# Four buffers instead of three for the split weights of a hybrid encoder layer, and half the transfer scratch

## The chip, the cores and the metric

The kernel runs on one core of a Trainium2 chip. The metric is the device time of one execution in microseconds (us). Beside it there is one profiled execution, whose trace is what the views below are taken from.

## What is computed

One layer of an encoder trunk, for 384 rows: 256 of a new stream and 8 × 16 of running streams. The model width is 2048.

```python
u = rmsnorm(x, g_mix_pre)
proj = u @ w_in                     # columns: pool | z | xBC | dt | gates
a_pool = pool_mixer(pool_in, ...)   # windows 2, 4, 8, 16, then pool_w
a_ssd = gated_rmsnorm(ssd_scan(causal_conv(xbc), ...), z, ssd_norm)
merged = gate_A * (a_pool @ w_pool_proj) + gate_B * (a_ssd @ w_ssd_proj)
x = x + rmsnorm(merged @ w_out, g_mix_post)
hdn = square(relu(rmsnorm(x, g_mlp_pre) @ w_up)) @ w_down
x = x + rmsnorm(hdn, g_mlp_post)
```

The new pool, convolution and scan states are outputs too.

## The kernel before

**Split products.** Every weight and every activation is float32 and is multiplied as a sum of a high part and a low part, both in the type float32r. `mm3` (L101 to L104) makes three matmuls of each product: high weight by high activation, high by low, low by high. So each weight unit of 128 × 1024 numbers goes through three steps. SyncE (SP) loads it into a raw tile `w` (`wfetch`, L64). ScalarE (ACT) writes the rounded copy `wh` (L71 in `wsplit`). VectorE (DVE) writes the rest, `wl` = `w` − `wh` (L72). `split` (L1206, L1207) does the same for the units of the two block products below, whose raw tiles come from another pool; `esplit` (L351, L353) does it for the first weights, and `chained` (L1753, L1754) for two units at the start of the last stage.

**Rings.** `wpool` holds three rings, `w`, `wh` and `wl`, each of three tiles of 4096 bytes in every partition. A tile can be written again only when its last reader is done. So `wh` and `wl` of unit n+3 wait for the last matmul of unit n, and `w` of unit n+3 waits for the DVE subtraction of unit n.

**Stages, in the order of time.** The projections of the pool part, the z part and the convolved x, B and C parts (`proj`, PSUM tiles `pj_p`, `pj_x`, `pj_z`), in eight rounds with the chunked scan between them. Their results go through two PSUM banks in turn (`mm` tiles), from which DVE reads them: `cbuf` (L436) for x, `zs` (L1099) for z. Then the two gates (`ga`, `gb`; `moving`, matmuls L155 to L157), with the block products `sq` of w_pool_proj and w_ssd_proj woven between their units. Then `wo` (w_out), then the MLP: `pj_up` (w_up) with the block products `wd` (w_down) woven in.

**Block products.** `quad` multiplies a 2 × 2 block of weight units with seven products instead of eight. Its seven forms are worked off in the order b11, b21, U, b22, W, V, X (L1259 to L1261 are the matmuls). U, W and X are sums of units. GpSimd (POOL) makes the first of these sums by a load that accumulates (L1219); DVE makes three more (L1246, `w_b` ← `w_b`, `w_b`). Partial sums are kept in `acc`: ACT copies them into a PSUM bank before the form that adds to it (L1231) and out again after it (L1236); DVE reads the others (L1238) and works off sums of finished blocks (L1286).

**Order.** The order of the instructions on each engine is fixed when the program is built. A scheduler places them by what they depend on, so that the number of tiles in a ring also moves instructions. `later` and `behind` keep some instructions behind the latest split.

Of the kernel before, what the change touches and what calls it, by code (L numbers as in the profile page):

```python
# [7 lines left out]
F32R = mybir.dt.float32r  # L8
# [6 lines left out]
P = 128  # L15
# [9 lines left out]
WINDOWS = (2, 4, 8, 16)  # L25
MAGIC = 1597463007.0
NWARM = 6

C_IDENT, C_ONES, C_MASK, C_CM, C_BM = 0, 128, 256, 768, 1024
C_RC, C_SCAN, C_END = 1032, 1096, 1504  # L30
# [3 lines left out]
def build(ctx, tc, io):  # L34
    nc = tc.nc
# [3 lines left out]
    wpool = ctx.enter_context(tc.tile_pool(name="wpool", bufs=3))  # L39
# [13 lines left out]
    def sstile(name):  # L53
        return pss.tile([P, 512], F32, tag="ss", name=name)

    def behind(ins):
        return nullcontext() if ins is None else tc.issue_after(ins.ins)
# [3 lines left out]
    def wfetch(src, name):  # L61
        w = wpool.tile([P, 1024], F32, tag="w", name=f"w_{name}")
        with behind(ahead[0]):
            fetched[0] = sy.dma_start(w, src)  # L64
        return w, name

    def wsplit(f):
        w, name = f
        h = wpool.tile([P, 1024], F32R, tag="wh", name=f"wh_{name}")
        l = wpool.tile([P, 1024], F32R, tag="wl", name=f"wl_{name}")  # L70
        cut[0] = s.activation(h, w, AF.Copy)  # L71
        cut[1] = v.tensor_tensor(l, w, h.bitcast(F32), ALU.subtract)  # L72
        return h, l
# [9 lines left out]
    def wload(src, name):  # L83
        return wsplit(wfetch(src, name))
# [204 lines left out]
    wt = sstile("warm_o")  # L289
    for _ in range(NWARM):  # L290
        te.matmul(wt, warm[:, :P], warm, start=True, stop=True)
# [30 lines left out]
    def xsplit(k):  # L322
        x = xr[k]
        h = xgp.tile([P, T], F32R, name=f"xgh{k}")
        l = xgp.tile([P, T], F32R, name=f"xgl{k}")
        g1 = x0[:, k : k + 1]
        s.activation(h, x, AF.Copy, scale=g1)
        xg.append((h, l))
        return v.scalar_tensor_tensor(
            out=l, in0=x, scalar=g1, in1=h.bitcast(F32), op0=ALU.mult, op1=ALU.subtract  # L330
        )
# [5 lines left out]
    def esplit(k):  # L337
        w = eu[k]
        n = 1 if k < 4 else 2
        h = wpool.tile([P, 1024], F32R, tag="wh", name=f"wh_e{k}")[:, : n * 512]  # L340
        l = wpool.tile([P, 1024], F32R, tag="wl", name=f"wl_e{k}")[:, : n * 512]
        hv, lv = (h, l) if n == 1 else (a.rearrange("p (k n) -> p k n", k=2) for a in (h, l))
        xl = None
        if k < 2:
            m = (P, 256)[k]
            with behind(low[0]):
                v.tensor_copy(hv[:, :m], w[:, :m])
            xl = xsplit(k)
            turn[0] = s.activation(hv[:, m:], w[:, m:], AF.Copy)
        else:  # L350
            turn[0] = s.activation(hv, w, AF.Copy)  # L351
        with behind(xl):
            low[0] = v.tensor_tensor(lv, w, hv.bitcast(F32), ALU.subtract)  # L353
        return h, l
# [25 lines left out]
    for k in range(4):  # L380
        if k > 1:
            xsplit(k)
        eprod(k, 0, esplit(k))
    for k in range(4, KD, 2):
        xsplit(k)
        xsplit(k + 1)
        hl = esplit(k)
        eprod(k, 0, hl)
        eprod(k + 1, 1, hl)
        if k in (10, 14):  # L390
            square((k - 10) // 4, turn[0])
    ps4 = sstile("pj_p4")[:, :T]
    early.append(ps4)
    half(ps4, 0, wsplit(f0), xg)
    square(2, None)
    half(ps4, 1, wsplit(f1), xg)
    dgh = pa.tile([P, 3, P], F32R, name="dgh", bufs=1)
    dgl = pa.tile([P, 3, P], F32R, name="dgl", bufs=1)
# [49 lines left out]
    with tc.tile_pool(name="phc", bufs=1, reuse_waits="tile") as pc, tc.tile_pool(name="phc2", bufs=2, reuse_waits="tile") as pc2:  # L448
# [5 lines left out]
        bufs = []  # L454
# [746 lines left out]
        return acc[:, nb // 2 * 9 + LEFT[b, nb % 2], :]  # L1201

    def split(w, name):
        h = wpool.tile([P, 1024], F32R, tag="wh", name=f"wh_{name}")
        l = wpool.tile([P, 1024], F32R, tag="wl", name=f"wl_{name}")
        cut[0] = s.activation(h, w, AF.Copy)  # L1206
        cut[1] = v.tensor_tensor(l, w, h.bitcast(F32), ALU.subtract)  # L1207
        return h, l

    def quad(nm, pool, acc, np_, fresh, unit, part, extra=lambda i: None, seeded=SEEDED):  # L1210
# [29 lines left out]
        def ready(f):  # L1240
            if f == ORDER[0] and not kept:
                load()
            wh, wl = split(kept[f], f"{f}_{nm}")
            if f in AHEAD:
                n, o, x, y, op = AHEAD[f]
                v.tensor_tensor(kept[o], kept[x], kept[y], op)  # L1246
                kept[n] = kept[o]
            return wh, wl
# [323 lines left out]
    with tc.tile_pool(name="phf", bufs=1, side="right", reuse_waits="tile") as pf, tc.tile_pool(  # L1572
        name="phf2", bufs=2, side="right", reuse_waits="tile"
# [9 lines left out]
        def act(fn):  # L1583
            with behind(ca[0]):
                ca[0] = fn()

        def dve(fn):
            with behind(cd[0]):
                cd[0] = fn()
# [158 lines left out]

        def chained(src, name):
            w, _ = wfetch(src, name)  # L1750
            h = wpool.tile([P, 1024], F32R, tag="wh", name=f"wh_{name}")
            l = wpool.tile([P, 1024], F32R, tag="wl", name=f"wl_{name}")
            act(lambda: s.activation(h, w, AF.Copy))  # L1753
            dve(lambda: v.tensor_tensor(l, w, h.bitcast(F32), ALU.subtract))  # L1754
            return h, l
# [37 lines left out]
        prod((0, 1), (6, 7))  # L1793
        prod((0,), range(8, 16))
        uw.append(chained(io["w_up"][1, 1], "up1_1"))
        prod((1,), range(8, KD))
        chain[0] = False
        for b, i in ((1, 2), (1, 3), (2, 0), (2, 1), (2, 2), (2, 3)):
            square(b, i)
        for b in range(3):  # L1800
            gp.dma_start(x1_scr[b], x1[:, b, :])
        u20 = chained(io["w_up"][2, 0], "up2_0")
        dgh = pf.tile([P, 3, P], F32R, name="dgh2")
        dgl = pf.tile([P, 3, P], F32R, name="dgl2")
# [21 lines left out]
    with tc.tile_pool(name="phg", bufs=1, side="right", reuse_waits="tile") as pg, tc.tile_pool(  # L1826
        name="phg2", bufs=2, side="right", reuse_waits="tile"
# [72 lines left out]
        for G4 in range(2 * NC):  # L1900
# [5 lines left out]
            for f4 in range(4):  # L1906
                f = G4 * 4 + f4
# [38 lines left out]
        for src, name in wd_units(3):  # L1946
            w, _ = wfetch(src, name)
            h = pg2.tile([P, 1024], F32R, tag="ff", name=f"eh_{name}", bufs=2)
            l = pz.tile([P, 1024], F32R, name=f"el_{name}")
# [3 lines left out]
        for b in range(3):  # L1953
            t = slice(b * P, b * P + P)
            for i in range(2):
                for k in range(4):
                    wh, wl = kept[i * 2 + k // 2]
# [141 lines left out]
```

## Time and profile before

| | us |
|---|---|
| median of three runs (lowest, highest) | 2579.84 (2579.22, 2581.45) |
| the profiled execution's own time | 2579.85 |
| its span, first to last instruction | 2578.1 |
| TensorE matmuls busy | 2562.9 |
| VectorE busy | 2031.0 |
| ScalarE busy | 1696.9 |
| GpSimd busy | 466.5 |

The span is 1.75 us shorter than the time of the same execution. PE is TensorE's matmuls and PEld its weight loads, DVE is VectorE, ACT ScalarE, POOL GpSimd, SP SyncE. In a timeline row stand the start in the span, the time taken, the engine, the line, what is written ← what is read and, in brackets, how long the engine had been idle and what ended that. A PE row's length is that of a pipelined matmul: the next one starts before it ends.

### The profile page before, as it was taken

The page shows a single profiled execution, that of the slowest core. Times are in us where ns is not written, and L with a number is a line of the kernel's source. Part 1 is how long each engine was busy: PE and PEld are TensorE (multiplying, and loading weights), DVE is VectorE, ACT ScalarE, POOL GpSimd, SP SyncE. Part 2 cuts the span into 40 slices and gives each one's busy share as a digit, 9 for nine tenths or more (in the row PEclk, how much of TensorE's full clock was granted, in tenths as well). Part 3 has the DMA queues.
Part 4 walks back from the last instruction along what each step waited for, and adds up shares of the span by engine and source line. Part 5 has one row for each costly group of instructions (what it writes and reads, how often), then busy time and mean ns, then how long its engine had stood idle before and what let it go on. Part 6 is the DMA issues. An engine that isn't in the chain of part 4 may idle for free.

```text
span 2578.1 us, 40110 instructions
## 1 busy us (share of the span) xinstructions
PE 2562.9 (99%) x14953; PEld 2387.1 (93%) x14953; DVE 2031.0 (79%) x2843; ACT 1696.9 (66%) x2683; POOL 466.5 (18%) x695
## 2 busy tenths in 40 slices
PE   9999999999999999999999999999999999999998
PEld 9999999999999988888888888999999999999997
DVE  6887889999999966898888855767777776777778
ACT  6545666666666546868888634666766666666665
POOL 0113445444544412211111100000000000000000
PEclk9999999999999999999999999999999999999999
DMA  7666767676767659977666545654555554555544
GB/s 286 207 220 224 238 218 231 216 242 224 232 216 244 225 181 313 290 233 218 199 189 200 189 168 191 211 157 147 156 160 167 166 161 148 155 157 166 159 156 155
DMA packets 150098, 516.57 MB, mean 200 GB/s; under 512 B 22432, under 2 KB 25312, under 8 KB 144656
## 3 DMA queue, kind: packets, MB, share of 16 engines
q1 hardware_dynamic: 98944, 355.14, 41.2%
q0 software_dynamic: 43904, 144.07, 19.3%
q10 hardware_dynamic: 7056, 14.81, 1.8%
q8 instruction: 117, 1.92, 0.3%
q14 instruction: 77, 0.63, 0.1%
HBM read 453.57 MB, written 60.36 MB: 199 GB/s over the span
## 4 chain that ended last, share of the span: by engine, by line
PE 91%; DVE 4%; issue 2%; ACT 1%; DMA 1%; POOL 0%; SPq 0%; DVEq 0%; ACTq 0%; POOLq 0%
PE pj_up L102 6%; PE pj_up L104 6%; PE pj_up L103 6%; PE wd L1260 6%; PE wd L1261 6%; PE wd L1259 6%; PE pj_x L102 5%; PE pj_x L103 5%; PE pj_x L104 5%; PE pj_z L104 3%; PE pj_z L103 3%; PE pj_z L102 3%; PE sq L1260 3%; PE sq L1261 3%; PE sq L1259 3%
## 5 line engine op out<-in xcount | busy, mean ns | idle before, releaser
L71 ACT ACTIVATE wh_up<-w_up 128x1024 fp32r<-128x1024 f32 x126 | 133.1, 1057 | 219.6 <-PE pj_up L103 202.5
L102 PE MATMUL pj_x<-xgh,wh_x 128*128 128x384 f32 x768 | 251.9, 328 | 0.9 <-DVE zs L1099 0.9
L102 PE MATMUL pj_up<-x1h,wh_up 128*128 128x384 f32 x768 | 250.5, 326 | 0.0
L103 PE MATMUL pj_x<-xgl,wh_x 128*128 128x384 f32 x768 | 250.4, 326 | 0.0
L104 PE MATMUL pj_x<-xgh,wl_x 128*128 128x384 f32 x768 | 250.4, 326 | 0.0
L103 PE MATMUL pj_up<-x1l,wh_up 128*128 128x384 f32 x768 | 250.4, 326 | 0.0
L104 PE MATMUL pj_up<-x1h,wl_up 128*128 128x384 f32 x768 | 250.4, 326 | 0.0
L72 DVE TENSOR_TENSOR wl_up<-w_up,wh_up 128x1024 fp32r<-128x1024 f32 x126 | 153.9, 1222 | 54.9 <-ACT wh_up L71 54.8
L1219 POOL DMA_DIRECT2D w_b_wd<-w_down x30 | 25.3, 843 | 832.9 <-DMA w_b_wd<-w_down 414.0
L102 PE MATMUL pj_z<-xgh,wh_z 128*128 128x384 f32 x512 | 166.9, 326 | 0.0
L103 PE MATMUL pj_z<-xgl,wh_z 128*128 128x384 f32 x512 | 166.9, 326 | 0.0
L104 PE MATMUL pj_z<-xgh,wl_z 128*128 128x384 f32 x512 | 166.9, 326 | 0.0
L102 PEld LDWEIGHTS pj_x<-xgh,wh_x 128*128 128x128 f32 x768 | 145.1, 189 | 3.1 <-DVE zs L1099 1.4
L103 PEld LDWEIGHTS pj_up<-x1l,wh_up 128*128 128x128 f32 x768 | 145.2, 189 | 1.2
L102 PEld LDWEIGHTS pj_up<-x1h,wh_up 128*128 128x128 f32 x768 | 145.2, 189 | 1.2
L103 PEld LDWEIGHTS pj_x<-xgl,wh_x 128*128 128x128 f32 x768 | 145.2, 189 | 0.0
L104 PEld LDWEIGHTS pj_x<-xgh,wl_x 128*128 128x128 f32 x768 | 145.2, 189 | 0.0
L104 PEld LDWEIGHTS pj_up<-x1h,wl_up 128*128 128x128 f32 x768 | 145.2, 189 | 0.0
L1236 ACT COPY acc<-wd 128x512 f32<-128x512 f32 x214 | 124.7, 583 | 23.8 <-PE wd L1261 23.8
L71 ACT ACTIVATE wh_x<-w_x 128x1024 fp32r<-128x1024 f32 x96 | 100.4, 1051 | 60.6 <-PE pj_z L103 30.1
L1259 PE MATMUL wd<-wh_b_wd,fh 128*128 128x512 f32 x360 | 136.4, 379 | 0.0
L1260 PE MATMUL wd<-wl_b_wd,fh 128*128 128x512 f32 x360 | 136.4, 379 | 0.0
(495 smaller groups left out, 8169.0 us busy)
## 6 DMA issues: line engine op xcount, KB each, us to landing
w_up<-w_up SPq DMA_DIRECT2D x128, 512.0 KB, 4.0
w_b_wd<-w_down SPq DMA_DIRECT2D x120, 512.0 KB, 4.2
w_x<-w_in SPq DMA_DIRECT2D x96, 512.0 KB, 4.0
w_z<-w_in SPq DMA_DIRECT2D x64, 512.0 KB, 4.2
w_b_sq<-w_ssd SPq DMA_DIRECT2D x64, 512.0 KB, 5.1
w_ga<-w_ga SPq DMA_DIRECT2D x32, 512.0 KB, 3.4
hs<-ssm POOLq DMA_DIRECT2D x16, 1024.0 KB, 6.2
new_ssm_s<-hs POOLq DMA_DIRECT2D x16, 1024.0 KB, 4.2
```

Source lines behind the costliest of these rows:

```text
L71: cut[0] = s.activation(h, w, AF.Copy)
L72: cut[1] = v.tensor_tensor(l, w, h.bitcast(F32), ALU.subtract)
L102: te.matmul(out, wh, xh, start=first, stop=False, **how)
L103: te.matmul(out, wh, xl, start=False, stop=False, **how)
L104: return te.matmul(out, wl, xh, start=False, stop=last, **how)
L1219: summed[0] = gp.dma_start(w, unit(0, np_ * 2), accum_op=ALU.add)
L1236: s.copy(dst, o)
L1259: te.matmul(out, mh, vh, start=begin, stop=False, skip_group_check=held)
L1260: te.matmul(out, mh, vl, start=False, stop=False, skip_group_check=held)
L1261: te.matmul(out, ml, vh, start=False, stop=end, skip_group_check=held)
```

## The change

The rings `wh` and `wl` get four tiles each instead of three, wherever they are allocated; the ring `w` keeps three. That takes 2 × 4096 = 8192 more bytes in every partition. They come from the space that the program's builder keeps free in every partition for the transfers that POOL issues, 16384 bytes unless told otherwise and 8192 now.

```diff
+NR = 4
...
     def wsplit(f):
         w, name = f
-        h = wpool.tile([P, 1024], F32R, tag="wh", name=f"wh_{name}")
-        l = wpool.tile([P, 1024], F32R, tag="wl", name=f"wl_{name}")
+        h = wpool.tile([P, 1024], F32R, tag="wh", bufs=NR, name=f"wh_{name}")
+        l = wpool.tile([P, 1024], F32R, tag="wl", bufs=NR, name=f"wl_{name}")
         cut[0] = s.activation(h, w, AF.Copy)
         cut[1] = v.tensor_tensor(l, w, h.bitcast(F32), ALU.subtract)
         return h, l
...
-    nc = bacc.Bacc("TRN2", target_bir_lowering=False, num_devices=1)
+    nc = bacc.Bacc("TRN2", target_bir_lowering=False, num_devices=1, dynamic_dma_scratch_size=8192)
```

`esplit`, `split` and `chained` are changed as `wsplit` is. The lines of the changed kernel are one higher than those of the kernel before (L71 becomes L72).

The amount of work on every engine stays as it was, and SP's loads and PE's matmuls keep nearly the same order. What moves are the splits on ACT and DVE. The first place is ACT in the woven stage, around the split of the form U of a block product (`wh_U_sq_1`); `wh_b_sq` are splits of plain units, `acs<-sq` copies out of PSUM, `sq_1_4<-acs` copies into it. Before:

```order
L71 ACTIVATE wh_gb_2_12490<-w_gb_2_12488 128x1024
L1236 COPY acs<-sq_1_0_12426 128x512
L1231 COPY sq_1_4_12471<-acs 128x512
L1231 COPY sq_1_2_12517<-acs 128x512
L1206 ACTIVATE wh_U_sq_1_12512<-w_b_sq_1_12438 128x1024
L1231 COPY sq_1_5_12533<-acs 128x512
L1236 COPY acs<-sq_1_1_12451 128x512
L1206 ACTIVATE wh_b_sq_1_12528<-w_b_sq_1_12445 128x1024
```

Now:

```order
L72 ACTIVATE wh_gb_2_12490<-w_gb_2_12488 128x1024
L1237 COPY acs<-sq_0_3_12403 128x512
L1207 ACTIVATE wh_U_sq_1_12512<-w_b_sq_1_12438 128x1024
L1237 COPY acs<-sq_1_0_12426 128x512
L1232 COPY sq_1_4_12471<-acs 128x512
L1232 COPY sq_1_2_12517<-acs 128x512
L1207 ACTIVATE wh_b_sq_1_12528<-w_b_sq_1_12445 128x1024
L1232 COPY sq_1_5_12533<-acs 128x512
L1237 COPY acs<-sq_1_1_12451 128x512
```

The split of U has moved ahead of three copies, that of the plain unit ahead of two; the copy out of `sq_0_3`, which stood ahead of the gate's split before, now stands behind it.

The second place is DVE further on in that stage, up to the low part of the gate's unit 4 (`wl_gb_4`); `w_b_sq<-w_b_sq,w_b_sq` is a sum of units. Before:

```order
L1207 TENSOR_TENSOR wl_U_sq_0_13512<-w_b_sq_0_13457,wh_U_sq_0_13511 128x1024
L1246 TENSOR_TENSOR w_b_sq_0_13457<-w_b_sq_0_13457,w_b_sq_0_13464 128x1024
L1337 TENSOR_TENSOR aV_13526<-ax_13222,aV_13526 128x256
L1246 TENSOR_TENSOR w_b_sq_0_13460<-w_b_sq_0_13457,w_b_sq_0_13460 128x1024
L1238 TENSOR_TENSOR acs<-sq_0_7_13446,acs 128x512
L72 TENSOR_TENSOR wl_gb_4_13532<-w_gb_4_13529,wh_gb_4_13531 128x1024
```

Now:

```order
L1208 TENSOR_TENSOR wl_U_sq_0_13512<-w_b_sq_0_13457,wh_U_sq_0_13511 128x1024
L1338 TENSOR_TENSOR aV_13526<-ax_13222,aV_13526 128x256
L1247 TENSOR_TENSOR w_b_sq_0_13457<-w_b_sq_0_13457,w_b_sq_0_13464 128x1024
L73 TENSOR_TENSOR wl_gb_4_13532<-w_gb_4_13529,wh_gb_4_13531 128x1024
L1247 TENSOR_TENSOR w_b_sq_0_13460<-w_b_sq_0_13457,w_b_sq_0_13460 128x1024
```

The gate's low part now stands ahead of one sum of units and one reading of PSUM.

The third place is DVE in the first scan round, up to the reading of the first z projection (`zs_0`); `cacc` is the convolution, `xb` a transposition. Before:

```order
L710 STREAM_TRANSPOSE xb_2701<-xs_2616 128x384
L72 TENSOR_TENSOR wl_x_0_2796<-w_x_0_2793,wh_x_0_2795 128x1024
L685 SCALAR_TENSOR_TENSOR cacc_2875<-cbuf_649,vec,cacc_2875 128x384 x2
L72 TENSOR_TENSOR wl_x_1_2826<-w_x_1_2823,wh_x_1_2825 128x1024
L685 SCALAR_TENSOR_TENSOR cacc_2875<-cbuf_649,vec,cacc_2875 128x384
L710 STREAM_TRANSPOSE xb_2957<-xs_2880 128x384
L1099 TENSOR_TENSOR zs_0_2853<-pj_z_0_2792,rstd 128x384
```

Now:

```order
L73 TENSOR_TENSOR wl_x_0_2796<-w_x_0_2793,wh_x_0_2795 128x1024
L711 STREAM_TRANSPOSE xb_2701<-xs_2616 128x384
L73 TENSOR_TENSOR wl_x_1_2826<-w_x_1_2823,wh_x_1_2825 128x1024
L686 SCALAR_TENSOR_TENSOR cacc_2875<-cbuf_649,vec,cacc_2875 128x384 x2
L73 TENSOR_TENSOR wl_z_1_0_2900<-w_z_1_0_2897,wh_z_1_0_2899 128x1024
L686 SCALAR_TENSOR_TENSOR cacc_2875<-cbuf_649,vec,cacc_2875 128x384
L711 STREAM_TRANSPOSE xb_2957<-xs_2880 128x384
L1100 TENSOR_TENSOR zs_0_2853<-pj_z_0_2792,rstd 128x384
```

One more split (`wl_z_1_0`) stands ahead of the reading of `pj_z`.

More of the change, by code (lines that the diff above doesn't have):

```diff
@@ L339, in esplit @@
         n = 1 if k < 4 else 2
-        h = wpool.tile([P, 1024], F32R, tag="wh", name=f"wh_e{k}")[:, : n * 512]
-        l = wpool.tile([P, 1024], F32R, tag="wl", name=f"wl_e{k}")[:, : n * 512]
+        h = wpool.tile([P, 1024], F32R, tag="wh", bufs=NR, name=f"wh_e{k}")[:, : n * 512]
+        l = wpool.tile([P, 1024], F32R, tag="wl", bufs=NR, name=f"wl_e{k}")[:, : n * 512]
         hv, lv = (h, l) if n == 1 else (a.rearrange("p (k n) -> p k n", k=2) for a in (h, l))
@@ L1203, in split @@
     def split(w, name):
-        h = wpool.tile([P, 1024], F32R, tag="wh", name=f"wh_{name}")
-        l = wpool.tile([P, 1024], F32R, tag="wl", name=f"wl_{name}")
+        h = wpool.tile([P, 1024], F32R, tag="wh", bufs=NR, name=f"wh_{name}")
+        l = wpool.tile([P, 1024], F32R, tag="wl", bufs=NR, name=f"wl_{name}")
         cut[0] = s.activation(h, w, AF.Copy)
@@ L1750, in chained @@
             w, _ = wfetch(src, name)
-            h = wpool.tile([P, 1024], F32R, tag="wh", name=f"wh_{name}")
-            l = wpool.tile([P, 1024], F32R, tag="wl", name=f"wl_{name}")
+            h = wpool.tile([P, 1024], F32R, tag="wh", bufs=NR, name=f"wh_{name}")
+            l = wpool.tile([P, 1024], F32R, tag="wl", bufs=NR, name=f"wl_{name}")
             act(lambda: s.activation(h, w, AF.Copy))
```

## The prediction

> **What bounds the kernel now.** I read the page first, then the stretches, then what PE waited for.
>
> ```profile
> span 2578.1 us, 40110 instructions
> ...
> PE 2562.9 (99%) x14953; PEld 2387.1 (93%) x14953; DVE 2031.0 (79%) x2843; ACT 1696.9 (66%) x2683; POOL 466.5 (18%) x695
> ```
>
> PE is the bound: it stands idle for only 2578.1 − 2562.9 = 15.2 us. The change takes no matmul away, so it can only win back idle time. The stretches, with PE's busy time first behind the length, tell where that is.
>
> ```profile
> core 0: us, PE busy (x) PEld busy (x) DVE busy (x) ACT busy (x) POOL busy (x), PEclk, DMA share, GB/s
> 0.00:250.00 250.00, 248.27 (x1465) 240.97 (x1465) 192.14 (x374) 133.86 (x229) 36.84 (x75) 1.00 0.70 236
> 250.00:251.00 1.00, 0.36 (x2) 0.36 (x3) 1.00 (x3) 0.86 (x2) 1.00 (x3) 1.00 0.91 307
> 251.00:940.00 689.00, 689.00 (x5170) 668.95 (x5169) 614.21 (x936) 438.15 (x815) 306.51 (x426) 1.00 0.68 225
> 940.00:1110.00 170.00, 169.56 (x780) 146.41 (x779) 121.81 (x120) 117.87 (x166) 36.65 (x61) 1.00 0.89 278
> 1110.00:1410.00 300.00, 296.31 (x1351) 253.52 (x1351) 262.07 (x311) 247.56 (x384) 41.60 (x68) 1.00 0.68 204
> 1410.00:1610.00 200.00, 199.94 (x972) 174.99 (x971) 132.51 (x177) 103.16 (x161) 13.78 (x25) 1.00 0.57 188
> 1610.00:2560.00 950.00, 950.00 (x5180) 893.94 (x5179) 693.29 (x892) 651.80 (x919) 30.09 (x39) 1.00 0.53 161
> 2560.00:2578.00 18.00, 9.44 (x44) 7.94 (x42) 13.93 (x35) 3.63 (x11) 0.00 (x0) 0.87 0.49 175
> ```
>
> The end (8.56 us idle behind the last matmul) and most of the start (1.73) have nothing to do with the rings. The MLP (950.00 of 950.00) and the scan rounds behind the first (689.00 of 689.00) leave nothing to win. What is left lies at 250 us (0.64) and from 940 to 1610 us: 0.44 + 3.69 + 0.06 = 4.19 us, nearly all of it where gate `gb` and the block products `sq` are woven. Who ends it:
>
> ```profile
> PE gb L156 <- DVE wl_gb L72: 2.6, 7, 0.6
> PE warm_o L291 <- DVE warm L287: 1.2, 1, 1.2
> PE pj_x L102 <- DVE zs L1099: 0.9, 1, 0.9
> PE sq L1260 <- DVE wl_V_sq L1207: 0.4, 1, 0.4
> PE ga L156 <- DVE wl_ga L72: 0.3, 1, 0.3
> PE pj_p L367 <- ACT xgh L327: 0.3, 1, 0.3
> PE sq L1260 <- DVE wl_b_sq L1207: 0.2, 1, 0.2
> ```
>
> Ten waits (7 + 1 + 1 + 1) for a low part, 2.6 + 0.4 + 0.3 + 0.2 = 3.5 us of idle time. That is not their whole price. The longest one on PE:
>
> ```profile
> 1120.63 0.38 PE L1261 MATMUL sq<-wh_W_sq,aW 128*128 128x512 f32 x1
> 1120.84 0.59 PE L155 MATMUL gb<-wh_gb,xgh 128*128 128x512 f32 x2
> 1122.01 0.48 PE L156 MATMUL gb<-wl_gb,xgh 128*128 128x512 f32 x1 [0.57 <-DVE wl_gb L72]
> 1122.33 0.38 PE L157 MATMUL gb<-wh_gb,xgl 128*128 128x512 f32 x1
> ```
>
> Matmuls overlap: they start 0.21 us apart (1120.63, 1120.84), though each row is 0.38 long. From 1120.84 to 1122.33 there are three steps, 0.64 us undisturbed and 1.49 here. The wait cost 0.85 us, 0.28 more than its idle time.
>
> **The change part by part: the fourth tile.** Why was that low part late? ACT and DVE in the twelve us before:
>
> ```profile
> 1109.75 1.06 ACT L1206 ACTIVATE wh_U_sq<-w_b_sq 128x1024 fp32r<-128x1024 f32 x1
> 1111.98 1.06 ACT L1206 ACTIVATE wh_b_sq<-w_b_sq 128x1024 fp32r<-128x1024 f32 x1 [0.17 <-PE sq L1261]
> 1115.86 1.06 ACT L1206 ACTIVATE wh_W_sq<-w_b_sq 128x1024 fp32r<-128x1024 f32 x1 [2.52 <-PE gb L157]
> ```
>
> ```profile
> 1110.85 1.23 DVE L1207 TENSOR_TENSOR wl_U_sq<-w_b_sq,wh_U_sq 128x1024 fp32r<-128x1024 f32 x1 [0.89 <-ACT wh_U_sq L1206]
> 1120.74 1.22 DVE L72 TENSOR_TENSOR wl_gb<-w_gb,wh_gb 128x1024 fp32r<-128x1024 f32 x1
> ```
>
> ACT stood 2.52 us because the tile it wanted to write still belonged to a gate unit that PE was working on: the ring was full. DVE stood 0.89 us for the split of U, and from 1110.85 on it worked without a break until `wl_gb` was done at 1121.96 (no row between shows an idle time). A start 0.6 us earlier would have been enough. With four tiles each of these splits waits for the unit before, whose matmuls end one unit earlier: 6 matmuls × 0.215 = 1.3 us for the shortest forms, 18 × 0.215 = 3.9 us for a gate unit. In the new order on ACT the split of U also stands ahead of three copies of about 0.58 each. So here DVE's 0.89 us pause can be closed, which is more than the 0.57 that PE stood. How often ACT is held like this from 1050 to 1410 us (the two largest of six such rows), and in the MLP:
>
> ```profile
> ACT wh_b_sq L1206 <- PE gb L157: 12.3, 8, 3.0
> ACT wh_V_sq L1206 <- PE gb L157: 7.4, 3, 2.9
> ACT wh_up L71 <- PE pj_up L103: 202.5, 104, 2.8
> ```
>
> In 11 waits of these two rows alone ACT stood 19.7 us for the ring. The wait in the MLP is far greater, and PE lost nothing there: a full ring costs only where DVE has no time to make it good. From 1110 to 1410 DVE works 262.07 us of 300, ACT 247.56. With PE's waits gone the stretch would be some 294 us long, and DVE would be 89% busy, ACT 84%: enough in the mean, though not in every burst.
>
> The sum. Ten waits: 3.5 + 10 × 0.28 = 6.3 us. The stretches hold 4.19 − 3.5 = 0.69 us more idle time in waits too short for a row of their own; if each is 0.1 us, seven of them cost up to 0.69 + 7 × 0.28 = 2.6 us. So 8.9 us is the most that can be won there, and nothing the least if the new order makes as much new waiting. I take 6.2 us, seven tenths, because the low parts that PE waited for also move ahead of other DVE work in the new order (`wl_gb_4` ahead of a sum of 1.22 and a reading of 0.68), while a burst can still be late where the cause isn't the ring, such as a raw tile that lands late.
>
> **The wait at 250 us.** This one is a PSUM bank, not a split: the z projection must have been read before the bank is written again.
>
> ```profile
> 248.26 0.62 DVE L685 SCALAR_TENSOR_TENSOR cacc<-cbuf,vec,cacc 128x384 f32<-128x384 f32 x1
> 250.06 0.52 DVE L1099 TENSOR_TENSOR zs<-pj_z,rstd 128x384 f32<-128x384 f32 x1
> ```
>
> In the new order one more split, `wl_z_1_0` (1.22, as the low part above), stands ahead of the last `cacc`, behind which ACT's work, the transposition and `zs` follow. If the chain before starts as it did, PE's wait grows by 1.2; if the earlier splits and loads bring the chain forward by as much as the wait's 0.9 + 0.28, it goes. I take nothing and keep −1.2 and +1.2 for the range.
>
> **The rest.** The MLP and the later scan rounds are at nothing: PE waits for nothing there. What hides the changed order is the lead; if it went, the price is a split's 1.06 on ACT or 1.22 on DVE at each place. Behind the last matmul there is no split left to wait for: nothing. Loads of raw tiles follow the subtractions, so they come earlier or at the same time.
>
> **The smaller transfer space.** POOL's queue is in use throughout:
>
> ```profile
> q0 software_dynamic: 43904, 144.07, 19.3%
> ...
> 241.53 0.62 POOL L715 DMA_DIRECT2D t_scr<-xb  x1 [1.78 <-DMA hs<-ssm]
> L1219 POOL DMA_DIRECT2D w_b_wd<-w_down x30 | 25.3, 843 | 832.9 <-DMA w_b_wd<-w_down 414.0
> ```
>
> Once POOL had to stand 1.78 us before it could issue, until an earlier transfer had landed. With less space that might happen oftener. Bounds: nothing, or 1.78 us more before each of the 30 accumulating loads of the MLP, 53 us, if nothing covered it. The last row speaks for nothing: POOL stands idle for 832.9 us before these 30 anyhow, 27.8 each, so 1.78 is lost in that. A gain isn't excluded, but no row shows where it would be. The Trainium skill speaks against this part: "SBUF — State Buffer", section "SBUF size: 192, 224, or 256?", says that 16 KiB of every partition are set aside for the ring of these descriptors, and "DMA: Bandwidth & Descriptors", section "Terms", that one takes 16 B; by these the ring would fall from 1024 places to 512 (an estimate), and the sum would be up to 2573.7 + 53 if POOL fills it; by the row it stays. No run so far shows a full ring.
>
> **Sum.** 2579.85 (the profiled execution, 0.01 above the median) − 6.2 = 2573.7 us.
>
> **The rivals.**
>
> *A part of the waits stays* (2574.7 to 2578.8, likeliest 2577). DVE is the real limit in the bursts: the row at 1120.74 ends eleven us of unbroken work. If half of the 6.3 goes, 3.1 us are won. For it speaks DVE's 262.07 of 300, against it that in each burst DVE or ACT stood for the ring first.
>
> *Nothing changes* (2579.8). The ring of raw tiles keeps three, and a split needs its raw tile too: then the fourth tile stands empty. Against it: the rows name PE's matmuls as what ACT waited for, not a DMA.
>
> *Slower: splits ahead of the copies PE needs.* In the new order splits pass copies into PSUM (`sq<-acs`), without which a form can't begin.
>
> ```profile
> 1064.54 1.12 ACT L1231 COPY sq<-acs 128x512 f32<-128x512 f32 x2
> 1065.58 1.06 ACT L1206 ACTIVATE wh_X_sq<-w_b_sq 128x1024 fp32r<-128x1024 f32 x1
> 1066.11 0.38 PE L1259 MATMUL sq<-wh_V_sq,aV 128*128 128x512 f32 x1
> ```
>
> The first of these two copies ends at about 1065.1 and PE uses it at 1066.11, a lead of 1.0. One split of 1.06 ahead of it takes the lead away; two make PE wait 2.12 − 1.0 = 1.1, with the hidden part 1.4 us. There are 24 such places (12 groups, two halves). If half of them fell so: 12 × 1.4 = 17 us, with 6.2 won and 1.2 lost at 250 us 2579.85 + 17 − 6.2 + 1.2 = 2592. It decides from about 8 places on. Against it: ACT is idle before such copies anyhow, because the copies out of PSUM wait for PE, and the moved split fits there.
>
> *Slower: the transfer space.* 2580 to 2633, from the point at which the accumulating loads come later than POOL's 27.8 us of idle time per load.
>
> **How the numbers follow.** A run of this kernel can be told from no change at about 0.2%, 5.2 us (2574.7 and 2585.0). The forecast, 5.2 to 8.9 us won: 0.53. A part of the waits stays: 0.28. Nothing changes: 0.09. Splits ahead of the copies: 0.07. The transfer space: 0.03. So faster 0.53, same 0.37, slower 0.10. The range starts at 2579.85 − 8.9 − 1.2 = 2569.8 and reaches over the two cases of little gain to 2580.2, that is 0.4 above no change for the bank at 250 us where little is won; outside lie the slower cases and a rest.
>
> **What would show it.** Right: PE's idle time from 1110 to the end of the gates falls from 3.69 to below 1.2 us, the row `gb <- wl_gb` goes or shrinks below 1 us, ACT's waits for `gb` L157 shorten, the MLP stays without idle time, and the end stays at 8.6 us. Wrong: PE waits with `sq <- ACT` on a copy (the copies), `wh_U <- DMA w_b_sq` on ACT (the transfer space), `wl_gb` rows of the old size behind unbroken DVE work (a part stays), or a row at 250 us above 2 us.

## The result, and the profile after

The changed kernel takes 2568.58 us (median of six runs, 2568.12 to 2569.04) against 2580.06 of the kernel before (six runs, 2579.19 to 2581.45): a ratio of 0.9957, 95% interval 0.9947 to 0.9967. That is 11.5 us won where 6.2 were forecast, and 1.2 us below the lower end of the range.

The page of the kernel after:

```profile
span 2566.7 us, 40124 instructions
...
PE 2556.4 (100%) x14953; PEld 2389.6 (93%) x14953; DVE 2027.4 (79%) x2843; ACT 1690.2 (66%) x2683; POOL 456.1 (18%) x695
```

PE's idle time is 2566.7 − 2556.4 = 10.3 us, 4.9 less than the 15.2 of before. The span is 11.4 us shorter. So more than half of the gain was not idle time by this page. The stretches (same columns as in the prediction):

```profile
250.00:251.00 1.00, 1.00 (x8) 1.00 (x8) 0.97 (x4) 1.00 (x5) 1.00 (x2) 1.00 0.40 112
251.00:940.00 689.00, 689.00 (x5168) 668.85 (x5167) 610.68 (x933) 435.91 (x808) 294.91 (x425) 1.00 0.66 225
940.00:1110.00 170.00, 169.66 (x785) 147.72 (x784) 121.91 (x123) 119.22 (x169) 36.70 (x61) 1.00 0.86 276
1110.00:1410.00 300.00, 300.00 (x1391) 262.55 (x1391) 267.53 (x320) 254.59 (x399) 43.08 (x70) 1.00 0.70 212
1410.00:1610.00 200.00, 200.00 (x1007) 177.31 (x1006) 131.78 (x195) 102.05 (x176) 12.82 (x24) 1.00 0.52 178
1610.00:2558.00 948.00, 948.00 (x5138) 890.82 (x5136) 694.31 (x885) 639.88 (x894) 29.58 (x38) 1.00 0.53 162
2558.00:2567.00 9.00, 0.17 (x1) 0.00 (x0) 4.91 (x13) 0.98 (x3) 0.00 (x0) 0.79 0.52 181
```

The row to read is 1110 to 1410. PE's busy time rose by only 3.69 us, but in the same 300 us there are 1391 matmuls instead of 1351: 40 × 0.215 = 8.6 us more work. The busy time of the weight loads (PEld) shows it: 253.52 before, 262.55 now, 9.0 us more. The scan rounds and the MLP have no idle time in either kernel, and the end is as long as it was (PE idle for 8.5 of the last 8.7 us of the span, 8.6 before). What PE's matmuls still wait for, in the whole execution:

```profile
PE warm_o L292 <- DVE warm L288: 1.2, 1, 1.2
PE ga L157 <- DVE wl_ga L73: 0.3, 1, 0.3
PE pj_p L368 <- ACT xgh L328: 0.2, 1, 0.2
```

No row of `gb`, `sq` or `zs` is left. The gate unit that waited longest before (1120.84 to 1122.33) in the new trace, on PE and then on DVE:

```profile
1118.88 0.38 PE L156 MATMUL gb<-wh_gb,xgh 128*128 128x512 f32 x1
1119.10 0.38 PE L157 MATMUL gb<-wl_gb,xgh 128*128 128x512 f32 x1
1119.31 0.38 PE L158 MATMUL gb<-wh_gb,xgl 128*128 128x512 f32 x1
```

```profile
1113.10 1.22 DVE L1208 TENSOR_TENSOR wl_W_sq<-w_b_sq,wh_W_sq 128x1024 fp32r<-128x1024 f32 x1
1116.30 1.22 DVE L73 TENSOR_TENSOR wl_gb<-w_gb,wh_gb 128x1024 fp32r<-128x1024 f32 x1
```

The low part is done at 1117.5, 1.6 us ahead of the matmul that needs it at 1119.10. Before it was done at 1121.96, and the matmul started at 1122.01. ACT, however, still stands for gate units, and POOL's accumulating loads are as they were:

```profile
ACT wh_b_sq L1207 <- PE gb L158: 9.9, 7, 2.3
ACT wh_V_sq L1207 <- PE gb L158: 2.5, 1, 2.5
```

```profile
L1220 POOL DMA_DIRECT2D w_b_wd<-w_down x30 | 25.3, 844 | 828.2 <-DMA w_b_wd<-w_down 742.0
```

The two rows of ACT (1050 to 1410 us) were 12.3 in 8 and 7.4 in 3. The 844 ns of one load and the 828.2 us of idle time ahead of the 30 were 843 and 832.9.

### The profile page after: what moved, and what is told of

Same layout as the page of the kernel before. It is cut to its first block, busy times and chain, and to the rows that moved or that the text cites. A ratio compares the mean times of both kernels' runs of the same rounds, so it can differ in the third digit from the quotient of the medians.

```text
span 2566.7 us, 40124 instructions
## 1 busy us (share of the span) xinstructions
PE 2556.4 (100%) x14953; PEld 2389.6 (93%) x14953; DVE 2027.4 (79%) x2843; ACT 1690.2 (66%) x2683; POOL 456.1 (18%) x695
## 4 chain that ended last, share of the span: by engine, by line
PE 99%; DMA 1%; DVE 0%; ACT 0%; SPq 0%; DVEq 0%; issue 0%; ACTq 0%
PE pj_up L103 6%; PE pj_up L105 6%; PE pj_up L104 6%; PE wd L1262 6%; PE wd L1260 6%; PE wd L1261 6%; PE pj_x L103 5%; PE pj_x L104 5%; PE pj_x L105 5%; PE sq L1261 4%; PE sq L1260 4%; PE sq L1262 4%; PE pj_z L105 3%; PE pj_z L104 3%; PE pj_z L103 3%; PE wo L156 2%
## 5 line engine op out<-in xcount | busy, mean ns | idle before, releaser
L1220 POOL DMA_DIRECT2D w_b_wd<-w_down x30 | 25.3, 844 | 828.2 <-DMA w_b_wd<-w_down 742.0
L72 ACT ACTIVATE wh_up<-w_up 128x1024 fp32r<-128x1024 f32 x126 | 133.5, 1060 | 56.8 <-PE pj_up L104 36.1
L72 ACT ACTIVATE wh_x<-w_x 128x1024 fp32r<-128x1024 f32 x96 | 100.6, 1055 | 76.9 <-PE pj_z L104 39.3
L1208 DVE TENSOR_TENSOR wl_b_wd<-w_b_wd,wh_b_wd 128x1024 fp32r<-128x1024 f32 x90 | 110.0, 1222 | 48.4 <-ACT wh_b_wd L1207 48.4
L1207 ACT ACTIVATE wh_b_wd<-w_b_wd 128x1024 fp32r<-128x1024 f32 x90 | 95.4, 1060 | 79.5 <-PE pj_up L104 61.5
```

The lines of the kernel that those rows point to most:

```text
L1220: summed[0] = gp.dma_start(w, unit(0, np_ * 2), accum_op=ALU.add)
```

## The experiments

Each kernel ran beside the kernel before on the same chip, whose medians there were 2578.96 to 2579.10 us. An edit that is the same at several places is shown at one of them. The kernels with one or two more tiles have a scratch of 8192 bytes, those with three more 4096, thin sums 16384. Besides the time, one figure is used throughout: how much earlier (in us) PE starts the same matmul than in the trace of before, the matmuls counted from the first (56 of the 14953 stand elsewhere in the order at most). Between the matmuls that stood at 940 and at 1610 us before lies the stage of gates and block products; its gain is the difference. Each row comes from one execution. The column at 255 also holds differences of the first ten us: the 128×384 matmul that starts at 4.2 us takes 0.69 us in the trace of before and 0.43 in that of the change with ACT held, which is 1.70 us ahead by 30 us.

| | at 255 | at 940 | at 1610 | stage 940 to 1610 |
|---|---|---|---|---|
| the change | 0.93 | 0.93 | 11.23 | 10.30 |
| scratch alone | 0.97 | 0.97 | 1.23 | 0.26 |
| high 4, low 3 | −0.65 | −1.98 | 7.62 | 9.60 |
| high 3, low 4 | 0.39 | 0.39 | 0.28 | −0.11 |
| raw 4 | 0.62 | 0.62 | 0.63 | 0.01 |
| change, ACT and DVE held | 1.88 | 1.88 | 4.59 | 2.71 |
| all rings 4 | 2.65 | 2.64 | 12.88 | 10.24 |
| before, thin sums | 0.59 | 0.27 | 9.84 | 9.57 |
| high 5, low 3 | −6.93 | −69.52 | −61.01 | 8.51 |
| change, ACT held | 2.67 | −2.60 | −3.47 | −0.87 |
| change, DVE held | 1.26 | −3.91 | 4.18 | 8.09 |
| high 5, low 4 | 1.33 | −1.75 | 8.43 | 10.18 |
| high 5, raw 4 | 0.17 | −0.30 | 9.51 | 9.81 |

**The scratch alone.**

```diff
-    nc = bacc.Bacc("TRN2", target_bir_lowering=False, num_devices=1)
+    nc = bacc.Bacc("TRN2", target_bir_lowering=False, num_devices=1, dynamic_dma_scratch_size=8192)
```

> Only the transfer scratch of 8192 bytes; all rings keep three tiles and the order of instructions is that of before. Theory (the split tiles' ring is the whole cause): no change, 2580 +- 1.5 us, the waits of the gate for wl_gb as before (2.6 us in 7). Rival (part of the 11.5 us comes from the scratch or from where tiles lie in SBUF): below 2578 us. Rival (a smaller scratch costs something that the rings more than paid back): above 2582 us.

Measured: 2579.22 us, ratio 1.0001 (0.9992 to 1.0009). No change; the rivals about the scratch fall. What PE waited for:

```profile
PE gb L156 <- DVE wl_gb L72: 2.6, 7, 0.6
...
PE pj_x L102 <- DVE zs L1099: 0.2, 1, 0.2
```

The gate's waits are those of before. The wait for the bank at 250 us is not: 0.2 here and 0.9 before, with ACT and DVE in the same order. It changes from one execution to the next, so the 0.93 us that the changed kernel is ahead at 255 us can't be put down to the change.

**Four high tiles alone.**

```diff
-        h = wpool.tile([P, 1024], F32R, tag="wh", name=f"wh_{name}")
+        h = wpool.tile([P, 1024], F32R, tag="wh", bufs=4, name=f"wh_{name}")
```

> Four tiles for the high parts alone, three for the low parts. Theory (the split of unit n+3 on ScalarE was held by the ring, and VectorE behind it): the high part may be written earlier, but its low part still needs a free tile, which comes free with the same unit's matmuls, so VectorE is held at the same unit: little is won, 0 to 3 us, 2577 to 2580. Rival (VectorE's subtraction was late only because ScalarE's copies stood in line behind a held split; the low part's own tile is free in time): most of the gain, 2569 to 2572.

Measured: 2571.50 us, ratio 0.9969 (0.9956 to 0.9981). My theory fell, the rival held: the high parts' tile, with the order that comes with it, gives 9.60 of the 10.30 us in the stage. The total is 3 us behind the change; in the one execution traced this kernel loses 0.65 us before 255 and 1.3 more by 940.

```profile
PE pj_x L102 <- DVE zs L1099: 1.0, 1, 1.0
...
PE su L932 <- DVE xs L956: 0.7, 1, 0.7
```

DVE hardly waits for ACT's splits any more. Its largest row for them from 1000 to 1460 us, before and here:

```profile
DVE wl_b_sq L1207 <- ACT wh_b_sq L1206: 27.7, 31, 3.2
```

```profile
DVE wl_b_sq L1207 <- ACT wh_b_sq L1206: 6.0, 9, 1.0
```

All such rows together fall from 57.7 to 10.9 us: the high parts are ready earlier, and where DVE still stands it is mostly PE that releases it.

**Four low tiles alone.**

```diff
-        l = wpool.tile([P, 1024], F32R, tag="wl", name=f"wl_{name}")
+        l = wpool.tile([P, 1024], F32R, tag="wl", bufs=4, name=f"wl_{name}")
```

> Four tiles for the low parts alone; the order of instructions is that of before. Both theories: a low part can't be made before its high part, whose ring stays full, so nothing changes: 2580 +- 1.5 us. If it falls below 2577, the tile that VectorE waited for was the low part's own, and ScalarE's waits were without effect.

Measured: 2579.80 us, ratio 1.0003 (0.9994 to 1.0012). Nothing, as expected.

**Four raw tiles, high and low three.**

```diff
-        w = wpool.tile([P, 1024], F32, tag="w", name=f"w_{name}")
+        w = wpool.tile([P, 1024], F32, tag="w", bufs=4, name=f"w_{name}")
```

> Four raw tiles, three for the high and low parts: 4096 bytes more instead of 8192, with nearly the old order. Theory (ring of the split parts): no change, 2580 +- 1.5 us. Rival (units arrive late from DMA, and any earlier load helps): 2570 to 2577 us.

Measured: 2577.91 us, ratio 0.9994 (0.9986 to 1.0003); 0.01 us in the stage. The rival falls.

**The change with ACT and DVE held near the old order.** Each instruction of the two engines gets an order-only edge from a table of how before stood. Such an edge can hold an instruction behind older ones; it can't pull one ahead. The edit is shown against the changed kernel:

```diff
+    table = stood()
+    v, s = Kept(v, tc, table), Kept(s, tc, table)
```

> Rings of four as in the change, but ScalarE and VectorE held near the order of before by order-only edges (some 290 rows of the listing still differ on ScalarE and 90 on VectorE, against 1386 and 1172 in the change). Theory (the free tile does it, the moved rows don't): the woven stage keeps at least 7 of its 10 us, 2568 to 2573 us, and no gate waits for wl_gb. Rival (the moved splits do it: U ahead of three copies): at most 3 us, 2576 to 2580, with rows of wl_gb of about the old size.

Measured: 2575.50 us, ratio 0.9986 (0.9977 to 0.9995). Of the stage's 10.30 us only 2.71 are left, nearer to the rival, though the gate's waits for `wl_gb` are half as long as before (1.3 us in 4). Lines are 216 higher here than in the kernel before, and all rows of ACT and DVE in this stage carry the helper's line. What ACT waited for from 1000 to 1460 us, first in the kernel before, then held:

```profile
ACT wh_b_sq L1206 <- PE gb L157: 14.3, 9, 3.0
ACT acs L1236 <- PE sq L1261: 10.9, 37, 0.7
```

```profile
ACT acs L234 <- PE sq L1477: 67.6, 56, 3.1
```

The ring's waits are gone: the rows in which a split waits for PE come to 59.7 us before, and one is left here, `wh_gb <- PE gb`, of 1.2 us. But ACT stands as long as before (376.8 us busy of the 460, 380.4 in the kernel before), now at the copies out of PSUM that are in line ahead of the splits. The tile was free, but the split still stood behind the copies.

**All rings of four.** Against the changed kernel:

```diff
-        w = wpool.tile([P, 1024], F32, tag="w", name=f"w_{name}")
+        w = wpool.tile([P, 1024], F32, tag="w", bufs=4, name=f"w_{name}")
...
+    nc = bacc.Bacc("TRN2", target_bir_lowering=False, num_devices=1, dynamic_dma_scratch_size=4096)
```

> All three rings of four, and a scratch of 4096 bytes, half that of the change. Theory (after the change almost no wait for a split is left, and the scratch is without effect): 2567.5 to 2569, perhaps 0.3 less than the change for the one wait for wl_ga. Rival (the scratch fills up at POOL): above 2570, with POOL waiting before its loads for earlier transfers.

Measured: 2568.74 us, ratio 0.9959 (0.9946 to 0.9971), not to be told from the change. The wait for `wl_ga` stays at 0.3, and with a scratch of 4096 bytes no loss is seen either. No kernel tried here beats the change.

**Thin sums, rings of three.**

```diff
-                v.tensor_tensor(kept[o], kept[x], kept[y], op)
+                c = 64 if nm.startswith("sq") else 1024
+                v.tensor_tensor(kept[o][:, :c], kept[x][:, :c], kept[y][:, :c], op)
```

> Rings of three and the order of before, but VectorE's sums of units in the products sq take 64 of their 1024 columns, so the output is not the reference's; some 1.1 us less VectorE work for each sum. Theory (a full ring costs only where VectorE is in a burst, so that either a free tile or a shorter burst takes the wait away): 2569 to 2573 us, no row of wl_gb. Rival (the ring alone sets when a low part is ready, whatever VectorE does): 2577 to 2580, rows of wl_gb as before. Second rival (both bind in turn): 2573 to 2577.

Measured: 2570.23 us, ratio 0.9966 (0.9953 to 0.9978): the theory, but for one row of `wl_gb`, 0.3 us, that is left. The order is nearly that of before: 5 rows of ACT and 37 of DVE stand elsewhere, most of them the sums themselves. The stage from 1110 to 1410 us, and ACT from 1000 to 1460:

```profile
1110.00:1410.00 300.00, 299.74 (x1389) 262.16 (x1388) 229.08 (x320) 254.60 (x398) 43.01 (x70) 1.00 0.70 212
```

```profile
ACT wh_b_sq L1206 <- PE gb L157: 11.2, 9, 2.3
```

With DVE at 229 us instead of 262, PE does 1389 matmuls there, two fewer than with the change, although the rings are nearly as full as before (ACT still stands 11.2 us, 9 times, for this row; 14.3 in 9 before). So the full ring cost time here only through DVE's bursts. That the change wins by starting the bursts earlier doesn't follow from this run; four high tiles alone (above) and DVE held (below) speak for it.

**Five high tiles.**

```diff
-        h = wpool.tile([P, 1024], F32R, tag="wh", name=f"wh_{name}")
+        h = wpool.tile([P, 1024], F32R, tag="wh", bufs=5, name=f"wh_{name}")
```

> The same 8192 bytes spent otherwise: five tiles for the high parts, three for the low parts. Theory (it is ScalarE's tile that was short, and one more is enough): 2570 to 2572 us, as with four for the high parts alone, its losses before 530 us included, and the woven stage gains 10 us and no more. Rival (each further high tile takes more waits away): below 2568 us.

Measured: 2634.66 us, ratio 1.0213 (1.0199 to 1.0227): 56 us slower than before. The execution traced is the longest of the five (2641.17 us). The stage still gains 8.51 in it; the loss lies ahead of it, most of it in the scan rounds. What PE waited for, then one such place on ACT, DVE and PE:

```profile
PE cb L762 <- ACT xs L689: 22.4, 7, 4.7
PE su L932 <- DVE xs L956: 9.7, 6, 2.9
```

```profile
435.39 1.06 ACT L71 ACTIVATE wh_z<-w_z 128x1024 fp32r<-128x1024 f32 x1 [3.96 <-DMA w_z<-w_in]
...
436.60 0.62 ACT L683 ACTIVATE cacc<-cbuf,vec 128x384 f32<-128x384 f32 x1
439.21 0.62 ACT L689 ACTIVATE xs<-cacc,vec 128x384 f32<-128x384 f32 x1 [1.99 <-DVE cacc L685]
```

```profile
437.25 1.93 DVE L685 SCALAR_TENSOR_TENSOR cacc<-cbuf,vec,cacc 128x384 f32<-128x384 f32 x3 [4.31 <-ACT cacc L683]
```

```profile
439.88 0.88 PE L762 MATMUL cb<-xs,xs 128*128 128x256 f32 x2 [4.72 <-ACT xs L689]
```

A high tile is free, so the split `wh_z` stands early in ACT's line, but its raw tile has not landed: ACT stands 3.96 us at the head of its line, the convolution behind it starts late, DVE stands 4.31 us for that and PE 4.72. The same 5145 matmuls of the scan rounds in the kernel before, then here:

```profile
255.00:940.00 685.00, 685.00 (x5145) 664.95 (x5144) 610.99 (x929) 437.69 (x814) 304.72 (x423) 1.00 0.67 225
```

```profile
261.93:1009.52 747.59, 709.20 (x5145) 680.88 (x5144) 601.08 (x929) 432.18 (x805) 281.40 (x425) 0.97 0.62 207
```

62.6 us are lost, but PE is idle for only 38.4 of them; it is also busy 24.2 us longer with the same work. The column PEclk, the clock granted to PE, tells of most of that: 0.97 here, 1.00 before. Behind the wait of 4.72 us it is 0.50 from 440.30 to 443.70. There is such a stretch of 3.4 or 6.8 us at each of the ten waits of 1.65 us and more in these rounds, and none at the four from 1.27 to 1.30. Together they last 37.5 us; half of that, 18.8 us, is an estimate of what the clock cost. The next two kernels ask why the raw tile was late.

**Five high tiles with four low, and with four raw.** Against the kernel with five high tiles alone:

```diff
-        l = wpool.tile([P, 1024], F32R, tag="wl", name=f"wl_{name}")
+        l = wpool.tile([P, 1024], F32R, tag="wl", bufs=4, name=f"wl_{name}")
```

> Five high tiles, four low, three raw (scratch 4096 bytes). With five high and three low tiles, ScalarE stood 205 us from 260 to 940 us for raw tiles that had not landed. Theory A (chain: the raw tile of unit m can be loaded after the subtraction of m-3, which needs the low tile of m-6; one more tile in either ring breaks it): most of the 55 us lost goes, below 2585 us, and ScalarE's wait for DMA from 260 to 940 us falls below 100 us. Theory B (the low ring alone is out of step with the high ring): the same here, but not with a fourth raw tile. Theory C (with five high tiles the scheduler puts splits ahead of the work of the scan whatever the other rings are): stays above 2620 us.

```diff
-        w = wpool.tile([P, 1024], F32, tag="w", name=f"w_{name}")
+        w = wpool.tile([P, 1024], F32, tag="w", bufs=4, name=f"w_{name}")
```

> Five high tiles, three low, four raw (scratch 4096 bytes). Theory A (chain through the raw tile, see the run beside it): below 2585 us, ScalarE's wait for DMA from 260 to 940 us below 100 us. Theory B (the low ring is what is short): above 2620 us, with VectorE now waiting for low tiles. Theory C (the scheduler's order is the cause whatever the other rings are): above 2620 us, ScalarE's wait for DMA little changed or replaced by another wait ahead of the same scan work.

Measured: 2571.86 us, ratio 0.9973 (0.9963 to 0.9984), and 2570.65, ratio 0.9966 (0.9954 to 0.9978). Either tile brings the 56 us back. ACT's waits for raw tiles from 260 to 940 us, with five high tiles alone, then with the low tile, then with the raw tile:

```profile
ACT wh_x L71 <- DMA w_x<-w_in: 135.6, 59, 7.6
ACT wh_z L71 <- DMA w_z<-w_in: 69.2, 24, 6.3
```

```profile
ACT wh_x L71 <- DMA w_x<-w_in: 39.8, 23, 4.3
ACT wh_z L71 <- DMA w_z<-w_in: 32.0, 20, 3.4
```

```profile
ACT wh_x L71 <- DMA w_x<-w_in: 43.9, 20, 4.7
ACT wh_z L71 <- DMA w_z<-w_in: 20.6, 14, 3.7
```

204.8 us against 71.8 and 64.5 (69.5 with four high tiles alone, 19.9 before): theory A, the chain of raw, low and high tiles. The order is not the cause: with the fourth raw tile only 56 of ACT's 2683 rows and 22 of DVE's 2843 stand elsewhere than with five high tiles alone.

**The change with one engine held.** The wrappers are those of the kernel with both engines held; only the table is shorter. First it keeps ACT's 2655 entries of the 5496, so that DVE is free:

```diff
+    table = stood()
+    v, s = Kept(v, tc, table), Kept(s, tc, table)
```

> Rings of four, ScalarE alone held near the order of before (VectorE free to move; about 295 rows of ScalarE's listing differ from before, 696 of VectorE's). Theory (the moved splits on ScalarE bring the gain: the fourth tile is of little use while the split stands in line behind copies that wait for TensorE): the woven stage gains at most 4 us, as with both engines held; 2574 to 2577 us. Rival (VectorE's moved rows bring it: low parts ahead of sums of units): the woven stage gains at least 7 us; 2568 to 2572.

Then it keeps DVE's 2841, so that ACT is free, with the same two lines:

> Rings of four, VectorE alone held near the order of before (ScalarE free; about 1375 rows of ScalarE's listing differ from before, 186 of VectorE's). Theory (ScalarE's moved splits bring the gain): the woven stage gains at least 7 us; 2568 to 2572. Rival (VectorE's moved rows bring it): at most 4 us in the woven stage; 2574 to 2577.

Measured: ACT held 2585.49 us, ratio 1.0026 (1.0017 to 1.0035); DVE held 2577.72, ratio 0.9995 (0.9986 to 1.0003). Neither total came out as forecast, because each hold also loses some 5 us in the scan rounds (255 to 940 in the table: 5.27 and 5.17). The stage answers the question: −0.87 us with ACT held, 8.09 with ACT free. With both held it was 2.71, so DVE's new order beside ACT's old one costs time: one wait for `wl_b_sq` of 2.15 us, and behind it PEclk at 0.50 from 1171.30 to 1174.70, some 1.7 us (an estimate, half of 3.4). Two rows show the stage, from 1110 to 1410 us, of ACT held and of DVE held:

```profile
1110.00:1410.00 300.00, 295.81 (x1347) 253.95 (x1346) 260.23 (x310) 244.08 (x382) 40.46 (x66) 0.99 0.67 202
```

```profile
1110.00:1410.00 300.00, 299.50 (x1382) 260.10 (x1381) 265.91 (x318) 253.03 (x396) 43.04 (x70) 1.00 0.67 208
```

1347 matmuls are no more than the 1351 of before; 1382 are most of the way to 1391. With DVE held, its waits for ACT's splits from 1000 to 1460 us are 30.9 us, where the kernel before has 57.7: the splits come earlier. In the change itself they are 53.6; DVE's own order has moved there too, so this figure doesn't show what the earlier splits are worth there.

## Why the prediction was wrong

**The step that failed: "8.9 us is the most that can be won there", and behind it "it can only win back idle time".** Waits that leave PE no idle time were put at nothing. In the kernel before, from 1110 to 1410 us, steps between matmuls are longer than usual at 19 places, by 8.64 us together. 3.69 of these are idle time; the remaining 4.95 are 0.26 for each of the 19, close to the 0.28 that I took. But only nine of the 19 are in the rows of PE's waits (7 + 1 + 1), five more have a shorter idle time, and five have none. From 940 to 1610 us it is 37 places and 12.1 us: the ten waits with a row cost 6.55 us (I had 6.3), nine with a shorter idle time 2.96 (I had 2.6 at most), and 18 without any 2.63, for which the sum has no term. One of these:

```profile
1139.81 0.38 PE L155 MATMUL gb<-wh_gb,xgh 128*128 128x512 f32 x1
1140.15 0.48 PE L156 MATMUL gb<-wl_gb,xgh 128*128 128x512 f32 x1
1140.47 0.38 PE L157 MATMUL gb<-wh_gb,xgl 128*128 128x512 f32 x1
```

The second matmul starts 0.34 behind the first instead of 0.21, while the first, 0.38 long, still runs: no gap, no row. That it waited shows only in its 0.48 and in the late third: 0.23 us lost. After the change 2.1 us of late steps are left from 940 to 1610 us: 10.0 won, which the shift of PE's matmuls gives as 10.30. The same slip is in "A start 0.6 us earlier would have been enough": the late step at 1122.01 was 0.95 us instead of 0.21, so 0.74 were needed (DVE's pause of 0.89 covers it).

Two views of the kernel before would have shown it. One is the count: 1351 × 0.216 (the median step there) = 291.8 us of work in 300, so 8.2 lost where 3.69 were idle. The other is what the weight loader waited for, from 1110 to 1410 us:

```profile
PEld gb L156 <- DVE wl_gb L72: 6.3, 10, 1.0
PEld sq L1260 <- DVE wl_b_sq L1207: 2.3, 5, 0.5
PEld sq L1260 <- DVE wl_V_sq L1207: 1.2, 2, 0.8
PEld sq L1260 <- DVE wl_W_sq L1207: 0.9, 2, 0.5
PEld sq L1259 <- ACT wh_W_sq L1206: 0.5, 1, 0.5
PEld sq L1259 <- ACT wh_b_sq L1206: 0.2, 1, 0.2
```

Together 11.4 us in 21 waits: the places that the matmuls' rows leave out are here. The sum lies above the 8.64 that were lost, the matmuls' 3.2 far below. From 940 to 1610 us these rows come to 15.9 us (12.1 lost), after the change to 2.3 (2.1 lost). The Trainium skill, "Perfetto Trace Analysis", section "Identifying the Most-Contended Engine", says that matmul busy time is no good measure of how close a kernel is to the roofline, because pipelined instructions look smaller in the trace, and that the matmuls' share of the peak FLOPs and the busy share of the weight loads are to be used instead. The traces here agree that it misleads: matmul busy rose by 3.69 us in that stretch, weight-load busy by 9.0, the work by 8.6.

**Seven tenths.** I held back 0.3 for bursts that stay late. After the change 2.1 of 12.1 us are left, most of it in `ga` and `wo`; the woven part has 0.13 us from 1110 to 1410. This factor was too low as well: seven tenths of 12.1 would have been 8.5 us, 2.3 above the forecast, and the factor makes the other 1.5 up to 10.0.

**The mechanism** was right in its parts, but I gave the free tile too much of it and the moved order too little. The late low parts came from DVE's bursts (thin sums alone win 9.57 in the stage). The high parts' tile takes nearly all of them away (9.60), and DVE then waits far less for ACT's splits (10.9 us instead of 57.7): its work starts earlier. The tile works mostly by letting the scheduler move splits ahead of copies on ACT (8.09 with DVE held, 2.71 with both held). That low parts also pass other DVE work, on which the text leaned, is not needed for most of it. The opposite, the new order with three tiles, was not tried.

**The wait at 250 us** was taken at nothing. It is gone in the profile after and makes 0.9 of the 11.2 us by which that execution is shorter, but with the order unchanged it was 0.9 (before), 0.2 (scratch alone) and 0.4 (four low tiles) in three executions; what the change does to it can't be read from one.

**The rest** came as written: nothing in the later scan rounds, the MLP and the end, and nothing from the scratch.

**The rivals.** *A part of the waits stays*: no, 2.1 of 12.1 us. *Nothing changes* because raw tiles are the limit: no; a fourth raw tile wins 0.01 in the stage. *Splits ahead of the copies*: not with four tiles, since no row of PE's waits has `sq <- ACT`, the weight loader's rows have one of 0.2 us, and 0.13 us of late steps are left there. But it is the right fear. With five high tiles splits stood ahead of work that PE needs, in the scan rounds instead of the woven stage, and PE was 69.5 us behind by 940. *The transfer space*: no; with the smaller scratch alone the time was 2579.22 against 2578.96 us.

**What would show it** was right in four points of five: `gb` went, the idle time fell below 1.2 us, the MLP and the end stayed. ACT's waits for `gb` shortened only in part (12.3 to 9.9, 7.4 to 2.5), and the thin sums show that they need not shorten at all.

## What to carry to other kernels

Where matmuls overlap, price what a stage loses by its matmul count times the undisturbed step, and look at what the weight loader waits for; the matmuls' idle time showed 3.69 of 8.64 us here, because every wait cost more than its idle time and the shortest had none. Most of what the deeper ring won came because the instruction that it freed also moved forward in its engine's line (2.71 of 10.30 us without that). And a ring two tiles deeper than both of its neighbours let instructions stand at the head of the line for data that had not landed.

## What the runs showed that I had not expected

More room can cost far more than it wins: five high tiles instead of four take the kernel from 2571.5 to 2634.7 us, and one more low or raw tile takes it all back. A wait that isn't the ring's can be just as long: with the old order ACT stood 67.6 us at copies where it had stood at splits. A wait of PE can cost more than it lasts: at the longest of them with five high tiles the granted clock fell to half for 3.4 or 6.8 us, and the same work took 24.2 us more. And the wait for the bank at 250 us differs between executions of one order (0.9, 0.4 and 0.2 us), so a term of about 1 us can't be read from one profile.
